# Cutting mixed-width expert segments into equal pieces in a one-core MoE layer

## The chip, the cores and the metric

The kernel runs on one core of one Trainium2 chip. The metric is the device time of one execution in microseconds (us); lower is better.

## The reference, cut to what matters

One layer works on 512 tokens of width 1024. It normalises them, runs a recurrent head group and a long-convolution head group, merges the two, and then passes every token through two of 32 experts. The change lies in that last part:

```python
for e in range(N_EXPERTS):                       # 32 experts, each 1024 -> 512 -> 1024, f32
    ye = (jax.nn.silu(t @ w_gate[e]) * (t @ w_up[e])) @ w_down[e]
    out = out + combine[:, e:e + 1] * ye         # combine is nonzero for two experts of a token
```

Each expert has three matrices of 2 MB (gate, up and down), and every matrix must come from HBM once: 31 experts take part, 195 MB together. A final RMSNorm follows and gives the output.

## The kernel before

**Two phases.** In roughly the first 395 us of the profiled execution the kernel computes the mixing layer and the routing. The rest is the expert phase and a final norm of some 20 us.

**Segments and units.** Experts are sorted by how many tokens they may hold (`CAPS`, 32 to 192 tokens). An expert's tokens are cut into segments of 64 or 32. Segments are packed into units of 128 columns: two of 64, four of 32, or one of 64 and two of 32. A unit gathers its 128 tokens (matmuls of 128x128 bf16 with a one-hot matrix `R`), forms `g` and `u` (eight contraction steps each), multiplies them, transposes, forms `d` in two halves `h` of 512 output columns (four steps each, eight together), and scatters the result back by a one-hot matrix `PT` (matmuls of 128x512 with a `slot` tile as the stationary operand).

There are 14 units. By `ORDER` their groups run F1, F2, M1, M2, H1, M3, Q1, H2, Q2, A, M4, H3, Q3, where A is two units and every other group one. Q1, Q2 and Q3 have four segments of 32. **M4 and H3 have segments of 64, 32 and 32**; all others have two of 64. In M4 the three segments belong to three experts, in H3 the 64 and the first 32 to the same expert.

**The products.** `product` (L1870 and on) walks through the contraction steps. At each step it issues one f32 matmul per segment: the segment's 64 or 32 columns of the tokens are the stationary operand, 512 columns of that expert's weights are streamed, and `tile_position=(0, p0)` puts the segment on its own columns of the array. All of them write one PSUM bank at their own partitions. A chain of start-order edges keeps this sequence in any schedule.

**Weights.** A weight matrix comes in two loads of 1 MB (1024 KB), so an expert takes six. The loads go through a ring of 16 buffers in `slot` and `arena` memory, all issued by SyncE (the SP queue) in one fixed order by the line L1818: 12 for F1, 12 for F2, 12 for each M up to M3, 6 for H1 and H2, 24 for each Q, 12 for A, 18 for M4, 12 for H3. The sixteenth-next load cannot start before the matmuls that read the buffer have run.

**What sets the order.** A recorder notes every operation of the program and a list scheduler (`order`, `forward`, `backward`) places them all, in up to 25 passes, by its own cost table; engines then run in exactly that order. Every recorded operation shows the helper's line L560 (or L567), so tiles and shapes tell the operations apart. Because one plan covers the program, a change of any operation can move instructions everywhere.

Of the kernel before, what the change touches and what calls it, by code (L numbers as in the profile page):

```python
# [742 lines left out]
def kernel(ctx: ExitStack, tc: tile.TileContext, a: dict, out: bass.AP, dbg=None):  # L743
# [45 lines left out]
    def ps():  # L789
        if REC.direct:  # L790
            nbank[0] += 1
            return View.of(Mem((128, 512), F32, banks[nbank[0] % 8]))
        return View.of(Mem((128, 512), F32, bank=-1))
# [11 lines left out]
    def small(name, shape, dt=F32, bufs=1):  # L805
        if name not in rings:
            rings[name] = [0, [cst.tile(shape, dt, name=f"{name}{i}") for i in range(bufs)]]
        r = rings[name]
        r[0] += 1
        return r[1][r[0] % bufs]  # L810
# [807 lines left out]
    def bc(t, shape):  # L1618
        return t.to_broadcast(shape)
# [142 lines left out]
    for g_ in [[first[i:i + 2]] for i in range(0, len(first), 2)] + rest:  # L1762
        assert len(g_) <= 2
        groups.append([])
        for u in g_:
            p0, segs = 0, []
            for s, c in u:
                w = min(64, CAPS[s] - c)
# [83 lines left out]
    def expert_units(subs, need=lambda m: None, then=lambda: None, last=False):  # L1852
        bufs = [(nu[0] + j) % 2 for j in range(len(subs))]
        nu[0] += len(subs)
        for j, (segs, (n, R, iw), wks) in zip(bufs, subs):
            for kb in range(2):
                b = ps()
                for q in range(4):
                    k = 4 * kb + q
                    for r in range(4):  # L1860
                        for m in range(3):
                            T.matmul(b[:, q * n:q * n + n], xp[m][:, r, 128 * k:128 * k + 128], R[:, r, :n],
                                     start=r == 0 and m == 0, stop=r == 3 and m == 2)
                for q in range(4):
                    k = 4 * kb + q
                    xk, bk = XT[j][:, k, :n], b[:, q * n:q * n + n]
                    X.copy(xk, bk, scale=A2k[:, k:k + 1], bias=B2k[:, k:k + 1])
        then()

        def product(sub, m, lhs, parts, c0=0, nc_=512):  # L1870
            b, before = ps(), None
            for i, (k, kk, h) in enumerate(parts):
                for (p0, w), wv in zip(sub[0], sub[2]):
                    o = T.matmul(b[p0:p0 + w, :nc_], lhs[:, k, p0:p0 + w], wv(m, kk, h)[:, c0:c0 + nc_], start=i == 0,
                                 stop=i == len(parts) - 1, tile_position=(0, p0), skip_group_check=True)
                    if not REC.direct:

                        if before is not None:
                            o.preds.setdefault(before, None)
                        before = o.i  # L1880
            return b

        rows = [(k, k % 4, k // 4) for k in range(8)]
        need("g")
        for j, sub in zip(bufs, subs):
            n = sub[1][0]
            bg = product(sub, "g", XT[j], rows)
            S.activation(SG[j][:n], bg[:n], AF.Silu)
        need("u")
        for o in late:  # L1890

            o.like = len(REC.ops)
        late.clear()
        for j, sub in zip(bufs, subs):
            n, sg = sub[1][0], SG[j]
            bu = product(sub, "u", XT[j], rows)
            V.tensor_tensor(sg[:n], sg[:n], bu[:n], op=OP.mult)
            b = ps()
            for q in range(4):
                T.transpose(b[:, q * n:q * n + n], sg[:n, q * 128:(q + 1) * 128], ident[:n, :n])  # L1900
            S.activation(HT[j][:, :, :n], b[:, :4 * n].rearrange("p (q s) -> p q s", q=4), AF.Copy)
        need("d")
        for j, sub in zip(bufs, subs):
            n, R, iw = sub[1]
            iq = small("iq", [128, 4], bufs=2)
            V.scalar_tensor_tensor(iq[:n], bc(iw[:n, 0:1], [n, 4]), 0.25, quart[:n], op0=OP.mult, op1=OP.add)
            V.tensor_tensor(PT[:n], bc(iota[:n, None, :128], [n, 4, 128]), bc(iq[:n, :, None], [n, 4, 128]),
                            op=OP.is_equal)
            n0 = len(REC.ops)
            for h, c0, m in ((0, 0, 512), *((1, *p_) for p_ in (LASTP if last else ((0, 512),)))):  # L1910
                b = product(sub, "d", HT[j], [(k, k, h) for k in range(4)], c0, m)
                cs = slice(512 * h + c0, 512 * h + c0 + m)
                yp = ye[:n, c0:c0 + m]
                V.scalar_tensor_tensor(yp, b[:n, :m], iw[:n, 1:2], g2b[:n, cs], op0=OP.mult, op1=OP.mult)
                if m > 256:
                    S.activation(YH[:n, h, :m], yp, AF.Copy)
                    V.tensor_tensor(YL[:n, :m], yp, YH[:n, h, :m].bitcast(F32), op=OP.subtract)
                for r in range(4):
                    b = ps()
                    if m > 256:  # L1920
                        T.matmul(b[:, :m], PT[:n, r], YH[:n, h, :m], start=True, stop=False)
                        T.matmul(b[:, :m], PT[:n, r], YL[:n, :m], start=False, stop=True)
                    else:
                        T.matmul(b[:, :m], PT[:n, r].bitcast(F32), yp, start=True, stop=True)
                    xs = x2[:, r, cs]
                    V.tensor_tensor(xs, xs, b[:, :m], op=OP.add)
            late.extend(REC.ops[n0:])
# [8 lines left out]
    def need(gi, m):  # L1936

        ss = list(dict.fromkeys(s for i in groups[gi] for _, _, s, _ in units[i]))
        if gi == 1:
            todo = [(s, x, h) for s in ss for x in "gud" for h in range(2)]  # L1940
        else:
            todo = [(s, m, h) for h in range(2) for s in ss]
        for t in todo:
            if t not in loaded:
                loaded.add(t)
                load(*t, LASTP if gi == len(groups) - 1 and t == todo[-1] and m == "d" else ((0, 512),))
# [3 lines left out]
    for gi, g_ in enumerate(groups):  # L1950
        def then(nxt=groups[gi + 1:gi + 2]):
            for i in (nxt[0] if nxt else []):
                unit_place(i)
# [83 lines left out]
```

## Time and profile before

| | |
|---|---|
| median of 3 runs | 927.65 us (925.95 to 929.68) |
| the profiled execution | 931.36 us, of which the span is 929.6 us |
| outside the span | 1.76 us |
| TensorE busy | 855.6 us, 92% of the span |
| VectorE, ScalarE, GpSimd busy | 507.3, 279.9, 23.6 us |
| DMA | 259.73 MB, mean 279 GB/s |
| granted TensorE clock, mean | 0.971 of 2.4 GHz |

Times in the trace count from the start of the span. The tool records each f32 matmul of this kernel as two MATMULs (two passes), so a contraction step of a unit with four 32-wide segments is eight records. Matmuls on different columns of the array overlap in time, so the lengths of records don't add up; the distance from one step's start to the next is what a step costs.

### The profile page before, as it was taken

How to read it: one execution, taken by the hardware profiler on the slowest of the kernel's cores; microseconds unless marked ns; L12 is line 12 of the kernel's file. 1: busy time of each engine (PE TensorE's matmuls, PEld its weight loads, DVE VectorE, ACT ScalarE, POOL GpSimd, SP SyncE). 2: the span in 40 equal slices, each digit the busy share in tenths (PEclk: the TensorE clock that was granted, in tenths of full speed). 3: DMA queues.
4: the chain of work that ended last, by engine and by line, in shares of the span. 5: the costliest groups of instructions: out<-in, count | busy, mean ns of one | idle time of the engine just before them, and what ended most of it. 6: DMA issues, size and time to landing. Idle time of an engine off the chain costs nothing.

```text
span 929.6 us, 13429 instructions
## 1 busy us (share of the span) xinstructions
PE 855.6 (92%) x5282; PEld 453.6 (49%) x5283; DVE 507.3 (55%) x971; ACT 279.9 (30%) x511; POOL 23.6 (3%) x25
## 2 busy tenths in 40 slices
PE   3988998899999799599999999999999999999984
PEld 0344674578887577435544444453554323233332
DVE  7989889599999977604233322431413214212135
ACT  4678188764345124301211110120110100000014
POOL 0000001010003000000000000000000000000002
PEclk9989999799999899799999999999999999999997
DMA  9985377333423596398999989999999999876693
GB/s 292 414 276 195 103 238 218 135 118 120 148 80 131 187 327 223 119 361 306 367 386 386 386 294 359 388 386 386 386 387 386 386 387 382 321 281 223 231 335 142
DMA packets 132618, 259.73 MB, mean 279 GB/s; under 512 B 6928, under 2 KB 28432, under 8 KB 129606
## 3 DMA queue, kind: packets, MB, share of 16 engines
q1 hardware_dynamic: 132534, 258.81, 77.7%
q8 instruction: 43, 0.70, 0.3%
q14 instruction: 25, 0.20, 0.1%
q10 hardware_dynamic: 16, 0.02, 0.0%
HBM read 252.49 MB, written 6.31 MB: 278 GB/s over the span
## 4 chain that ended last, share of the span: by engine, by line
PE 68%; DVE 7%; DMA 1%; ACT 1%; issue 0%; SPq 0%; DVEq 0%; ACTq 0%
PE bank L560 68%; DVE arena L567 2%; DVE slot L567 2%; DVE arena L560 2%; DMA slot<-in_w_down_dram 1%; DVE slot L560 1%; ACT slot L560 0%; DVE R L560 0%; DVE rsb_in L560 0%; DVE fine L560 0%; ACT arena L560 0%; ACT slot L567 0%; SPq L1818 0%; DVE finy L560 0%; DVE hy L560 0%
## 5 line engine op out<-in xcount | busy, mean ns | idle before, releaser
L560 PE MATMUL bank<-arena 128*64 128x512 f32 (+8 forms) x1434 | 314.6, 533 | 26.0 <-DMA arena<-in_b_ada_dram 5.9
L560 PE MATMUL bank<-slot 128*128 128x512 f32 (+1 forms) x1064 | 282.8, 410 | 14.9 <-DVE slot L567 4.8
L560 PE MATMUL bank<-slot,arena 128*64 128x512 f32 (+2 forms) x936 | 242.9, 597 | 1.9 <-DMA slot<-in_w_down_dram 0.9
L560 PEld LDWEIGHTS bank<-slot 128*128 128x128 f32 x1064 | 195.2, 193 | 99.5 <-issue 27.3
L560 PEld LDWEIGHTS bank<-arena 128*32 128x32 f32 (+5 forms) x1434 | 100.5, 132 | 166.8 <-issue 117.5
L560 DVE TENSOR_TENSOR arena<-arena,bank 128x512 f32<-128x512 f32 (+2 forms) x131 | 80.5, 663 | 167.4 <-PE bank L560 167.2
L567 DVE TENSOR_TENSOR arena<-arena 128x512 f32<-128x512 f32 (+3 forms) x142 | 120.6, 886 | 2.5 <-DMA arena<-in_w_dram 1.8
L560 PEld LDWEIGHTS bank<-slot,arena 128*64 128x64 f32 (+1 forms) x936 | 58.3, 124 | 111.6 <-issue 101.0
L560 ACT ACTIVATE arena<-bank 128x512 f32<-128x512 f32 (+1 forms) x66 | 38.3, 595 | 243.4 <-PE bank L560 240.8
L560 PEld LDWEIGHTS <-slot 128*128 128x128 bf16 x1344 | 76.9, 98 | 40.9 <-issue 40.6
L560 PE MATMUL bank<-R,slot 128*128 128x128 bf16 x1344 | 88.7, 220 | 0.3 <-ACT arena L567 0.3
L567 DVE TENSOR_SCALAR arena<-bank,A2c,B2c 128x128 f32<-128x128 f32 x36 | 14.6, 410 | 115.6 <-PE bank L560 115.5
L567 ACT ACTIVATE arena<-bank,B2c,A2c 128x128 f32<-128x128 f32 x76 | 30.7, 454 | 137.1 <-DVE arena L567 85.4
L560 ACT ACTIVATE slot<-arena 128x512 fp32r<-128x512 f32 (+2 forms) x43 | 27.7, 645 | 113.5 <-DVE arena L560 104.2
L560 DVE SCALAR_TENSOR_TENSOR arena<-bank,iw,arena 128x512 f32<-128x512 f32 (+1 forms) x29 | 21.2, 732 | 69.6 <-PE bank L560 69.2
L560 PE MATMUL bank<-ident,arena 128*128 128x128 f32 (+2 forms) x234 | 40.7, 292 | 5.2 <-ACT arena L567 2.2
L560 ACT ACTIVATE arena<-arena 128x512 f32<-128x512 f32 (+6 forms) x59 | 32.7, 589 | 26.5 <-DVE arena L560 21.4
L560 PEld LDWEIGHTS bank<-ident,arena 128*128 128x128 f32 (+2 forms) x234 | 30.2, 160 | 19.9 <-issue 5.7
L567 ACT ACTIVATE slot<-slot 128x1024 fp32r<-128x1024 f32 (+1 forms) x32 | 26.4, 846 | 28.4 <-DVE slot L567 22.9
L567 DVE TENSOR_TENSOR slot<-slot 128x1024 fp32r<-128x1024 f32 (+1 forms) x35 | 33.7, 974 | 0.1
L560 ACT ACT_TABLE_LOAD x23 | 29.5, 1283 | 6.0 <-DMA arena<-in_pack_dram 4.6
L560 DVE TENSOR_TENSOR arena<-bank,arena 128x512 f32<-128x512 f32 (+1 forms) x42 | 27.7, 680 | 5.5 <-PE bank L560 3.1
(172 smaller groups left out, 417.3 us busy)
## 6 DMA issues: line engine op xcount, KB each, us to landing
arena<-in_w_down_dram SPq DMA_DIRECT2D x41, 1024.0 KB, 13.5
slot<-in_w_up_dram SPq DMA_DIRECT2D x39, 1024.0 KB, 14.0
slot<-in_w_gate_dram SPq DMA_DIRECT2D x32, 1024.0 KB, 13.6
arena<-in_w_gate_dram SPq DMA_DIRECT2D x30, 1024.0 KB, 11.8
arena<-in_w_up_dram SPq DMA_DIRECT2D x23, 1024.0 KB, 9.4
slot<-in_w_down_dram SPq DMA_DIRECT2D x20, 1024.0 KB, 10.3
arena<-in_w_ada_dram SPq DMA_DIRECT2D x32, 512.0 KB, 5.1
slot<-in_w_ada_dram SPq DMA_DIRECT2D x8, 1024.0 KB, 11.1
```

The source lines that it names most:

```text
L560: return self.rec.add(self.name, lambda: f(*[real(v) for v in args], **{k: real(v) for k, v in kw.items()}), outs, ins, cost, **x)
L567: return cost, lambda: f(*[real(v) for v in args], **{k: real(v) for k, v in kw.items()}), port
```

## The change

`product` now takes the smallest segment width of the unit, `one`, and cuts every segment into pieces of that width. A piece starts at partition `p` and uses the weights of the segment that it came from. In a unit whose segments are all equally wide, each segment is one piece and nothing changes. In M4 and H3 the 64-wide segment becomes two 32-wide pieces, so a step has four matmuls of 32 columns in place of one of 64 and two of 32.

```diff
             b, before = ps(), None
+
+            one = min(w for _, w in sub[0])
+            turns = [(p, one, wv) for (p0, w), wv in zip(sub[0], sub[2]) for p in range(p0, p0 + w, one)]
             for i, (k, kk, h) in enumerate(parts):
-                for (p0, w), wv in zip(sub[0], sub[2]):
+                for p0, w, wv in turns:
                     o = T.matmul(b[p0:p0 + w, :nc_], lhs[:, k, p0:p0 + w], wv(m, kk, h)[:, c0:c0 + nc_], start=i == 0,
```

**Place 1: TensorE, the end of the `g` product of unit M4.** `bank_70` (before) and `bank_74` (after) is the product's PSUM bank, `slot` and `arena` name where the weights lie, and the size is that of the output. Before:

```order
L560 MATMUL bank_70<-slot,arena 64x512
L560 MATMUL bank_70<-arena 32x512 x2
L560 MATMUL bank_70<-arena 64x512
L560 MATMUL bank_70<-slot,arena 32x512 x2
L560 MATMUL bank_70<-arena 64x512
L560 MATMUL bank_70<-slot,arena 32x512 x2
L560 MATMUL bank_73<-slot 128x512
```

After:

```order
L560 MATMUL bank_74<-arena 32x512 x2
L560 MATMUL bank_74<-slot,arena 32x512 x2
L560 MATMUL bank_74<-arena 32x512 x4
L560 MATMUL bank_74<-slot,arena 32x512 x2
L560 MATMUL bank_74<-arena 32x512 x2
L560 MATMUL bank_74<-slot,arena 32x512 x2
L560 MATMUL bank_70<-slot 128x512
```

The product keeps its place between the down products and the scatter (128x512 from `slot`) of unit A; a step is now four outputs of 32 rows, with no other width between them.

**Place 2: TensorE, the `u` product of unit H3.** Before, `bank_74` is `u`; the rows between are scatters of unit M4 (128x512):

```order
L560 MATMUL bank_73<-slot 128x512
L560 MATMUL bank_69<-slot 128x512
L560 MATMUL bank_74<-slot,arena 32x512 x2
L560 MATMUL bank_74<-slot,arena 64x512
L560 MATMUL bank_74<-slot,arena 32x512 x2
L560 MATMUL bank_68<-slot 128x512
```

After, `bank_70` is the end of H3's `g`, `bank_71` the start of its `u`, and `bank_72` gathers tokens for Q3:

```order
L560 MATMUL bank_72<-R_137,slot 128x128
L560 MATMUL bank_70<-slot,arena 32x512 x13
L560 MATMUL bank_71<-slot,arena 32x512 x3
L560 LDWEIGHTS slot
L560 MATMUL bank_72<-R_137,slot 128x128
```

The steps stand in runs of four, with few other instructions cut in; the runs of H3's `g` and `u` alternate with the gathers of the unit that follows.

**Place 3: the SP queue, in the first phase.** One piece of the difference; `gd`, `w_ada`, `w_u` and `x` belong to the mixing layer:

```order
+L560 DMA arena<-in_w_ada_dram 128x4x256 x3
+L560 DMA gd<-arena 128x512 x2
 L560 DMA slot<-in_x_dram 128x1024
-L560 DMA gd<-arena 128x512
-L560 DMA arena<-in_w_ada_dram 128x4x256
-L560 DMA gd<-arena 128x512
-L560 DMA arena<-in_w_ada_dram 128x4x256
-L560 DMA gd<-arena 128x512
-L560 DMA arena<-in_w_ada_dram 128x4x256
```

The plan of the first phase, which the edit does not touch, has been made anew too. The order of the expert weights' loads among themselves is the same.

## Rows read from the trace of the kernel before

**Rows 1.** The page: span, busy time, and DMA by 40 slices.

```profile
span 929.6 us, 13429 instructions
...
PE 855.6 (92%) x5282; PEld 453.6 (49%) x5283; DVE 507.3 (55%) x971; ACT 279.9 (30%) x511; POOL 23.6 (3%) x25
...
GB/s 292 414 276 195 103 238 218 135 118 120 148 80 131 187 327 223 119 361 306 367 386 386 386 294 359 388 386 386 386 387 386 386 387 382 321 281 223 231 335 142
```

**Rows 2.** Windows of the expert phase: busy us by engine, granted clock, DMA.

```profile
395.00:465.00 70.00, 70.00 (x482) 32.53 (x478) 18.75 (x41) 10.13 (x21) 0.00 (x0) 1.00 0.95 345
465.00:720.00 255.00, 253.94 (x2009) 118.44 (x2009) 81.98 (x168) 34.06 (x71) 0.00 (x0) 1.00 1.02 376
720.00:757.00 37.00, 37.00 (x172) 12.79 (x168) 8.96 (x16) 4.98 (x9) 0.00 (x0) 1.00 1.05 386
757.00:790.20 33.20, 32.90 (x106) 9.19 (x104) 11.35 (x18) 1.86 (x3) 0.00 (x0) 1.00 1.05 383
790.20:907.20 117.00, 113.73 (x659) 36.73 (x657) 26.38 (x45) 10.67 (x21) 0.00 (x0) 1.00 0.78 279
907.20:929.60 22.40, 9.96 (x77) 5.90 (x77) 12.02 (x46) 10.89 (x34) 4.97 (x4) 0.77 0.37 134
```

**Rows 3.** The chain that ended last, from 776 us on: start, length, what.

```profile
776.25 119.12 PE bank L560 x630
896.49 10.68 DMA slot<-in_w_down_dram
907.21 6.96 PE bank L560 x63
```

**Rows 4.** Waits of the SP queue, longest in total: us, times, longest.

```profile
SPq L1818 <- PE bank L560: 324.7, 109, 13.4
```

**Rows 5.** SP timeline: issue of expert weights from M4's first load on.

```profile
720.11 1.48 SPq L1818 DMA_DIRECT2D slot<-in_w_gate_dram  x1
...
765.12 2.38 SPq L1818 DMA_DIRECT2D arena<-in_w_down_dram  x1
768.33 5.10 SPq L1818 DMA_DIRECT2D arena<-in_w_gate_dram  x2
773.68 5.00 SPq L1818 DMA_DIRECT2D slot<-in_w_gate_dram  x2
784.43 12.58 SPq L1818 DMA_DIRECT2D slot<-in_w_up_dram  x4
...
809.10 0.38 SPq L1818 DMA_DIRECT2D arena<-in_w_gate_dram  x1
...
896.49 3.01 SPq L1818 DMA_DIRECT2D slot<-in_w_down_dram  x3
```

**Rows 6.** PE timeline, M4's `g` product: start, length, shape, records.

```profile
757.51 1.05 PE L560 MATMUL bank<-arena 128*32 128x512 f32 x4
758.49 1.07 PE L560 MATMUL bank<-slot,arena 128*64 128x512 f32 x2
759.49 1.05 PE L560 MATMUL bank<-arena 128*32 128x512 f32 x4
760.48 1.07 PE L560 MATMUL bank<-slot,arena 128*64 128x512 f32 x2
761.48 1.05 PE L560 MATMUL bank<-arena 128*32 128x512 f32 x4
```

**Rows 7.** PE timeline, H3's `u` product, its last six steps.

```profile
843.53 11.98 PE L560 MATMUL bank<-slot,arena 128*64 128x512 f32 x36
855.44 0.25 PE L560 MATMUL bank<-auxb,R 128*128 128x3 bf16 x4
```

**Rows 8.** PE timeline, a down product of Q3, with four segments of 32.

```profile
900.53 0.60 PE L560 MATMUL bank<-slot,arena 128*32 128x512 f32 x2
900.54 1.00 PE L560 MATMUL bank<-arena 128*32 128x512 f32 x2
900.96 0.60 PE L560 MATMUL bank<-slot,arena 128*32 128x512 f32 x2
900.97 1.00 PE L560 MATMUL bank<-arena 128*32 128x512 f32 x2
901.38 0.60 PE L560 MATMUL bank<-slot,arena 128*32 128x512 f32 x2
```

**Rows 9.** PE timeline, two-of-64 steps of unit A: all pieces of one width.

```profile
711.28 9.66 PE L560 MATMUL bank<-slot,arena 128*64 128x512 f32 x44
720.88 1.42 PE L560 MATMUL bank<-slot 128*128 128x512 f32 x5
```

**Rows 10.** PE timeline, one 32-wide matmul alone on the array.

```profile
667.40 1.05 PE L560 MATMUL bank<-slot,arena 128*32 128x512 f32 x2
668.37 0.50 PE L560 MATMUL bank<-slot 128*128 128x512 f32 x1
```

**Rows 11.** Groups of weight loads into the array, by form: busy us, mean ns.

```profile
L560 PEld LDWEIGHTS bank<-slot,arena 128*32 128x32 f32 x440 | 20.5, 110 | 40.1 <-issue 32.8 <-DMA slot<-in_w_ada_dram 2.6 <-DMA slot<-in_w_down_dram 1.7
```

**Rows 12.** Windows with a busy array fed by DMA, and with an idle one.

```profile
607.00:700.00 93.00, 91.94 (x826) 45.21 (x821) 25.16 (x52) 13.64 (x30) 0.00 (x0) 1.00 1.05 386
372.00:388.00 16.00, 4.87 (x54) 4.17 (x54) 13.83 (x53) 4.84 (x7) 0.39 (x2) 0.57 0.48 166
```

**Rows 13.** Timeline of the tail: after the last weights, and the first output store.

```profile
907.21 1.05 PE L560 MATMUL bank<-slot,arena 128*32 128x256 f32 x4 [0.86 <-DMA slot<-in_w_down_dram]
908.19 0.73 PE L560 MATMUL bank<-slot 128*128 128x512 f32 x2
908.73 2.52 DVE L560 TENSOR_TENSOR arena<-arena,bank 128x512 f32<-128x512 f32 x4 [2.67 <-PE bank L560]
...
919.93 4.47 SPq L560 DMA_DIRECT2D out_dram<-slot  x8
```

## The prediction

> **What bounds the kernel now.** I read the page first. TensorE is busy for 92% of the span, while the other engines stay under 56%. The GB/s line by slices runs at 386 to 388 for long stretches, and then drops to 321, 281, 223 and 231 near the end [rows 1]. So there are two candidates, the array and the weight stream. The windows tell which one holds where. From 465 to 790 us both are near full: the array has no idle time worth naming and the loads run at 376 to 386 GB/s. From 790.2 to 907.2 us the array is still busy for 113.7 of 117.0 us, but the loads run at 279 GB/s [rows 2]. In that stretch the array alone is the bound. The chain of waits says the same: 119 us of TensorE from 776 us on, then one weight load of 10.7 us, then the last matmuls [rows 3]. The SP queue confirms it from the other side: issues of expert weights (L1818) waited 324.7 us in 109 waits for matmuls to give buffers back [rows 4]. The reader should see there that loads are late because buffers come free late.
>
> Which work makes the array slow there? M4's first load is issued at 720.1 us and Q3's first at 809.1 us [rows 5], and M4's products start at 757 us [rows 6]. So M4 and H3, the two units that the edit touches, fill the stretch from 757 to about 875 us, just where the loads fall behind.
>
> **What a step costs.** In M4's `g`, the pattern of a pair of records of 64 and four of 32 repeats from 757.51 to 761.48 us in two steps, so a step takes 1.985 us [rows 6]. In H3's `u`, 36 records, six steps, lie between 843.53 and 855.44 us: 1.985 us again [rows 7]. In a unit with four segments of 32, the four matmuls of one pass start together, and the next pass starts 0.43 us later (900.53, 900.96, 901.38): 0.86 us for the two passes of a step [rows 8]. With two segments of 64, 44 records or 11 steps take 9.60 us, 0.87 us each [rows 9]. So equal widths share the array completely. In the mixed step the 64 goes alone, the two 32s go together, and each of the two changes of width adds about 0.13 us: 2 x 0.86 + 2 x 0.13 = 1.98.
>
> The Trainium skill ("TensorEngine Tiling (Array Packing)", Key Properties) says that a change of tiling mode drains the array, while tiles of one mode run independently. The 1.985 against 0.86 us agrees with it.
>
> **The change part by part.** *Array work.* M4 and H3 have 8 steps for `g`, 8 for `u` and 2 x 4 for `d`, so 48 steps together. Before: 48 x 1.985 = 95.3 us. After, each step is four matmuls of 32, the form of rows 8, so 48 x 0.86 = 41.3 us. That is 54.0 us less. It adds one matmul a step, 48 in all, which costs nothing of its own as long as the four lie side by side. If a run begins or ends inside a step, a piece may stand alone on the array, and that takes 0.97 us [rows 10]. The order shows about a dozen such places in M4's and H3's products, so at most 12 us come back. The array's saving is 42 to 54 us.
>
> *What the end gains.* The loads can't follow that far. From 757 to 907.2 us the array works 32.9 + 113.7 = 146.6 us; after the change 93 to 105 us are left. In the same time 33.2 us x 383 + 117.0 us x 279 GB/s = 45.4 MB arrive [rows 2], which at 386 GB/s needs 117.5 us. The array would be done 13 to 25 us ahead of its weights, so the weight stream becomes the bound, and the gain is what the stream can make up. Before 790.2 us there is nothing to make up, since it ran at 383 to 386. After it, 117.0 x 279 = 32.6 MB would take 84.6 us at 386 GB/s: 32.4 us less. In the longest stretch in which the ring worked beside a busy array the rate was 376 [rows 2]; at that the 32.6 MB take 86.8 us, 30.2 us less. I take 376, because a queue that waits now and then is what this kernel has shown over a long stretch.
>
> Can the loads be issued in time? The ring has 16 buffers, and a load takes about 2.7 us at 386 GB/s. At 765 to 784 us the queue issued only the first loads of H3, in bursts [rows 5]; each waited for M4's `g` and `u` to give a buffer back. After the change M4's `g` takes 7 us in place of 16, so these buffers come free before their turn. While the array waits for weights it consumes each load soon after it lands. With some five loads on their way (13 us of queue at 2.7 us each) about ten buffers are then free, an estimate. So I see no stall in that stretch.
>
> *The tail.* From the last landing at 907.2 us to the end are 22.4 us [rows 2, 3]. The last two down products, their scatters and the final norm stay. Two small effects oppose each other. The adds of the first half's scatter, 2.5 us on VectorE after the last landing [rows 13], can come earlier, since the array is no longer behind. On the other hand the array will pause between the last loads, and its clock can fall: where it was busy for 4.9 of 16 us, the granted clock was 0.57, so much of that stretch ran at 1.2 GHz [rows 12]. I leave the tail at 22.4 us.
>
> *The rest of the program.* The planner has placed everything anew, the first phase too, and the SP queue there has another order. No row prices that. I take nothing for it and let it widen the range by some 10 us, about 2.5% of that phase's 395 us; this width is a choice.
>
> **The sum.** 931.36 - 30.2 = 901.2 us for an execution like the profiled one. That one stands 3.7 us above the median, so against the median it is 927.65 - 30.2 = **897.5 us**.
>
> **The rivals.**
>
> *The stream also closes its earlier gaps (0.10).* From 395 to 465 us it ran at 345 GB/s [rows 2]. At 386 these 24.2 MB take 62.6 us, 7.4 us less. With the full 32.4 us, and 2.5 us from the tail, the time is 927.65 - 42.3 = 885 us. Against it: the units there are unchanged, so only a luckier order could do this.
>
> *Part of the gain is given back (0.19).* With idle time on the array its clock may fall in Q3 and in the tail, and the first phase may come out longer. The tail's 10 us of matmuls at half rate would cost about 7 us; with some 8 us in the first phase the gain shrinks to 15 us, 912 us. For it: the row of 0.57 above. Against it: from 607 to 700 us, which is a stretch of Q work with loads at full rate, the clock stayed at 1.00 and the array busy, because the planner fills the waits with gathers [rows 12].
>
> *The weight loads into the array don't hide (0.03).* Eight loads of 32 columns a step at 0.110 us each [rows 11] would, if nothing covered them, make the step 0.86 + 0.88 = 1.74 us. Then 48 x 0.245 = 12 us are saved, and the array stays the bound: 916 us. Against it: rows 8 have just this form, with its eight loads, at 0.86 us. The Trainium skill ("TensorE: Matmul & The Clock Gate", The mechanism, in the part on packing small matmuls) says that a weight load overlaps running matmuls only when its row group differs, which pieces side by side in columns don't fulfil; the trace disagrees, since the step of 0.86 us is the two passes alone.
>
> *The pieces take turns in time and not side by side (0.03; the other side).* If four pieces that stream the same expert's weights, or four short issues in a row, can't run together, a step is 4 x 0.97 = 3.9 us at the row of one 32-wide matmul alone [rows 10]. That is 48 x 1.9 = 91 us more on the array, and about 1019 us in all. It decides as soon as the step is over 1.985 us, that is when fewer than about two pieces run at a time. Against it: Q units run four at a time [rows 8]. In unit A, whose steps take 0.87 us [rows 9], the two segments of the first unit share one expert's weights.
>
> The forecast itself gets 0.65. The range of 886 to 911 us leaves out about 2 in 10: the low rival and the far part of the give-back. Within 0.5% of the time before (about what a measurement of this kernel can tell from no change) I see 0.02, slower 0.03 and faster 0.95.
>
> **What would show it.** In the profile after, M4's and H3's steps should start every 0.86 us. The slices between 780 us and the last weights should read about 380 GB/s or more, and the chain there should name DMA landings of expert weights, not only TensorE. TensorE's busy time should fall by some 45 us, with idle time whose releaser is DMA. The last weights should land near 877 us, some 22 us before the end. I am wrong if a step still takes 1.7 us or more, if the loads stay under 350 GB/s although the steps are fast (then buffers are the limit and not the stream), or if the first expert matmuls start some 10 us later than before, which would put the blame on the first phase.

## The result, and the profile after

The changed kernel takes 890.93 us (median of 4 runs, 890.72 to 891.2). The kernel before took 928.52 us beside it (925.95 to 929.68). The ratio is 0.960, with a 95% interval of 0.958 to 0.962: 37.6 us faster. That is inside the range, and 6.6 us below the time that was predicted.

The page of the changed kernel answers to [rows 1]:

```profile
span 888.9 us, 13625 instructions
...
PE 810.6 (91%) x5378; PEld 449.6 (51%) x5379; DVE 508.2 (57%) x980; ACT 273.9 (31%) x499; POOL 22.4 (3%) x26
...
GB/s 290 415 313 261 60 204 217 209 94 142 166 48 131 136 349 187 252 213 387 272 387 386 386 354 300 385 386 387 386 386 386 386 386 387 386 386 385 387 382 130
```

TensorE has 45 us less to do. The dip of the GB/s line near the end is gone: the stream stays at 382 to 387 up to the last slice but one.

The windows of the changed kernel, cut at the same events as [rows 2] (M4's products start at 748 us now, the last weights are used from 864.6 us on):

```profile
395.00:465.00 70.00, 70.00 (x494) 33.16 (x491) 23.62 (x50) 9.53 (x20) 0.00 (x0) 1.00 0.96 350
465.00:748.00 283.00, 281.94 (x2126) 127.73 (x2123) 85.34 (x172) 39.04 (x80) 0.00 (x0) 1.00 1.03 377
748.00:864.60 116.60, 106.53 (x854) 42.70 (x852) 36.80 (x64) 12.13 (x23) 0.00 (x0) 0.97 1.05 386
864.60:888.90 24.30, 11.48 (x84) 7.13 (x84) 12.52 (x47) 10.91 (x34) 4.96 (x4) 0.78 0.42 150
```

From 748 to 864.6 us the loads run at 386 GB/s, and the array has 10 us of idle time. What sets the end of this stretch shows in the chain of waits; compare [rows 3]:

```profile
759.18 55.73 PE bank L560 x504
...
850.59 13.99 DMA arena<-in_w_down_dram
864.63 8.48 PE bank L560 x70
```

The unbroken 119 us of TensorE before the last load are 56 us now. Between the lines shown the chain goes on through shorter pieces of TensorE (18 us), VectorE and ScalarE up to 838.7 us, and from there it runs through the issues of the SP queue and the last load. M4's `g` product on the timeline, against [rows 6]:

```profile
748.77 0.60 PE L560 MATMUL bank<-slot,arena 128*32 128x512 f32 x2
748.78 0.60 PE L560 MATMUL bank<-arena 128*32 128x512 f32 x2
749.20 0.60 PE L560 MATMUL bank<-slot,arena 128*32 128x512 f32 x2
749.21 0.60 PE L560 MATMUL bank<-arena 128*32 128x512 f32 x2
749.63 0.60 PE L560 MATMUL bank<-slot,arena 128*32 128x512 f32 x2
```

Four pieces start within 0.01 us, and the next pass 0.43 us later: 0.86 us a step, as in the units of four 32s [rows 8]. And the array now waits for weights in Q3's `u` and down products, of which the rows of before have one, of 0.86 us [rows 13]:

```profile
842.94 1.05 PE L560 MATMUL bank<-arena 128*32 128x512 f32 x2 [0.94 <-DMA arena<-in_w_up_dram]
845.65 1.05 PE L560 MATMUL bank<-arena 128*32 128x512 f32 x2 [1.67 <-DMA arena<-in_w_up_dram]
848.37 6.58 PE L560 MATMUL bank<-arena 128*32 128x512 f32 x26 [1.67 <-DMA arena<-in_w_up_dram]
...
864.63 1.05 PE L560 MATMUL bank<-arena 128*32 128x256 f32 x4 [1.66 <-DMA arena<-in_w_down_dram]
```

**Where the 40.7 us of the span went.** Three marks divide both spans: the issue of A's first load (686.10 before, 677.64 after), the first matmul on the last weights (907.21 and 864.63) and the end. The first part is 8.5 us shorter, the second 34.1 us (221.1 to 187.0), and the third 1.9 us longer. So the stretch that the edit touches gave about what was forecast (34.1 us, less 1.9 in the tail, for the 30.2), and the first part, which the edit doesn't touch, gave 8.5 us on top.

**The theories.** Mine: the faster steps relieve the array by 42 to 54 us, the stream lets some 32 us of it through (this limit is the cap below: the weights can't arrive sooner), and the earlier start comes from the new plan of the first phase. Rivals: the new order of the expert phase, not the pieces, gives the gain; or there is no cap, and the pieces save only some 32 us.

### The profile page after: what moved, and what is told of

It reads as the page before. It is cut to its first block, busy times and chain, and to the rows that moved or that the text cites. A ratio compares the mean times of both kernels' runs of the same rounds, so it can differ in the third digit from the quotient of the medians.

```text
span 888.9 us, 13625 instructions
## 1 busy us (share of the span) xinstructions
PE 810.6 (91%) x5378; PEld 449.6 (51%) x5379; DVE 508.2 (57%) x980; ACT 273.9 (31%) x499; POOL 22.4 (3%) x26
## 4 chain that ended last, share of the span: by engine, by line
PE 61%; DVE 11%; DMA 2%; SPq 1%; issue 1%; ACT 1%; ACTq 0%
PE bank L560 61%; DVE arena L567 4%; DVE arena L560 3%; DVE slot L567 2%; DMA arena<-in_w_down_dram 2%; SPq L1818 1%; DVE slot L560 1%; ACT slot L560 0%; DVE R L560 0%; DVE rsb_in L560 0%; DVE fine L560 0%; ACT arena L560 0%; DVE finy L560 0%; ACT arena L567 0%; DVE he L560 0%
## 5 line engine op out<-in xcount | busy, mean ns | idle before, releaser
L560 PE MATMUL bank<-arena 128*32 128x512 f32 (+7 forms) x1474 | 300.1, 536 | 31.8 <-DMA arena<-in_b_ada_dram 7.3
L560 PE MATMUL bank<-slot 128*128 128x512 f32 (+1 forms) x1064 | 276.5, 404 | 12.8 <-DVE slot L567 7.5
L560 PEld LDWEIGHTS bank<-slot 128*128 128x128 f32 x1064 | 191.8, 189 | 97.6 <-issue 29.9
L560 PE MATMUL bank<-slot,arena 128*32 128x512 f32 (+2 forms) x992 | 220.5, 595 | 1.0 <-DMA slot<-in_w_ada_dram 0.6
L560 PEld LDWEIGHTS bank<-arena 128*32 128x32 f32 (+4 forms) x1474 | 101.2, 132 | 157.6 <-issue 98.8
L560 PEld LDWEIGHTS bank<-slot,arena 128*32 128x32 f32 (+1 forms) x992 | 57.7, 122 | 87.7 <-issue 78.8
L567 ACT ACTIVATE arena<-bank,B2c,A2c 128x128 f32<-128x128 f32 x75 | 30.3, 454 | 138.6 <-DVE arena L567 83.8
L567 ACT ACTIVATE slot<-slot 128x512 fp32r<-128x512 f32 (+1 forms) x29 | 24.0, 839 | 28.8 <-DVE slot L567 23.1
L567 DVE TENSOR_TENSOR slot<-arena,slot 128x512 fp32r<-128x512 f32 (+5 forms) x25 | 27.8, 1113 | 1.9 <-ACT hy L560 1.3
```

Source lines behind the costliest of these rows:

```text
L560: return self.rec.add(self.name, lambda: f(*[real(v) for v in args], **{k: real(v) for k, v in kw.items()}), outs, ins, cost, **x)
L567: return cost, lambda: f(*[real(v) for v in args], **{k: real(v) for k, v in kw.items()}), port
```

## The experiments

Each kernel ran in several rounds beside the kernel before; a gain is against that. "The stretch" is the time from A's first load to the issue of the last expert load, 211.6 us in the kernel before and 181.0 us in the changed one. The expectations also measure from A's long run, the 44 records in a row of [rows 9], to the first matmul on the last weights: 195.9 us before (711.28 to 907.21) and 161.7 us in the changed kernel (702.95 to 864.63).

### The old plan with pieces, and the new plan without

In the first kernel the planner sees the old operations; only when one is issued does it become two (the edit is shortened):

```diff
+ one = min(w_ for _, w_ in sub[0])
+ if w > one:                       # what the planned operation issues
+     def cut(...):
+         for p in range(p0, p0 + w, one):
+             nc.tensor.matmul(b[p:p + one], lhs[:, k, p:p + one], ..., tile_position=(0, p))
+     o.fn = cut
```

> The plan is that of the kernel before, instruction for instruction; only when M4's and H3's 64-wide matmuls are issued, each becomes two of 32. Theory (the faster steps give the gain of the last stretch, up to what the weight stream can make up; the 8.3 us by which unit A started earlier in the changed kernel come from the new plan of the first phase): A's long run starts at about 711 us as before, the stretch from there to the last landing shrinks from 195.9 to 162 to 166 us, the tail stays at 22 to 24 us, and the time is some 30 to 33 us below before. Rival (the new order of the expert phase gives most of the gain, the pieces little): the stretch stays above 180 us and the gain under 15 us.

Measured: 898.0 us against 929.18, ratio 0.967 (0.965 to 0.969), 31.2 us faster. Windows of this kernel, from A's first load to the last, and from there to the end:

```profile
684.70:865.60 180.90, 168.11 (x1281) 69.91 (x1272) 54.13 (x103) 19.37 (x37) 0.00 (x0) 0.97 1.04 383
865.60:896.50 30.90, 16.58 (x124) 8.33 (x124) 13.97 (x49) 12.11 (x36) 4.98 (x4) 0.85 0.59 211
```

A's long run starts at 710.22 us and the last weights are used from 874.19 us on: 164.0 us, as expected of the theory. With the plan held fixed, the pieces alone give the whole of the stretch's gain (180.9 us, against 181.0 in the changed kernel). The rival that the new order of the expert phase does it falls.

The second kernel does the reverse: planned as pieces, issued whole (of the edit, the line that says what is issued).

```diff
- turns = [(p, one, wv) for ...]
+ turns = [(p, one, wv, w if p == p0 else 0) for ...]    # first piece issues all of w, second nothing
```

> The plan is that of the changed kernel, made for pieces; but where it has the two pieces of a 64-wide segment, the segment is issued whole at the first and nothing at the second. Theory: A's long run starts near 703 us as in the changed kernel, M4's and H3's steps take about 2 us again, the stretch to the last landing is back at 190 to 200 us, and the time is some 5 to 10 us below before: the part that the plan of the first phase gives by itself. Rival (the new order of the expert phase gives most of the gain): the stretch stays under 175 us and the gain is 25 us or more.

Measured: 938.84 us, 9.7 us slower than before (ratio 1.012, 1.009 to 1.014). A's long run starts at 702.38 us, so the first phase is indeed 9 us shorter here too. But the stretch is not back at its old length, it is longer:

```profile
677.10:903.00 225.90, 224.05 (x1185) 75.27 (x1177) 54.26 (x103) 19.16 (x37) 0.00 (x0) 1.00 0.83 305
```

My number was a miss: I expected a gain of 5 to 10 us. The plan that is made for pieces breaks runs inside a step, and with whole segments a pair of 32s is torn apart at such a place. The order of this kernel shows it in M4's `u` (`bank_71`; `L1883` issues the whole segment):

```
L560 MATMUL bank_71<-arena 32x512
L1883 MATMUL bank_71<-slot,arena 64x512
L560 MATMUL bank_71<-arena 32x512
L560 MATMUL bank_69<-slot 128x512
L560 MATMUL bank_74<-slot 128x512
L560 MATMUL bank_71<-arena 32x512
```

Each 32 stands alone between a 64 and other work, where two would share the array. In M4's and H3's products the trace of this kernel has 20 matmuls of 32 columns that start alone, ten torn pairs; the kernel before has none. At the 0.97 us of one alone [rows 10] and 0.86 us of a pair, ten pairs cost 10 x (2 x 0.97 - 0.86) = 10.8 us, an estimate, out of the 14.3 us by which the stretch is longer. The rest stays open. The rival falls here too: the new order gives nothing by itself.

### One unit at a time

```diff
- turns = [(p, one, wv) for (p0, w), wv in ... for p in range(p0, p0 + w, one)]
+ turns = [(p, one if cut else w, wv) for (p0, w), wv in ... for p in range(p0, p0 + w, one if cut else w)]
```

`cut` holds for M4 alone, or for H3 alone.

> Only unit M4 is cut into pieces, H3 keeps 64, 32 and 32. Theory: the array is relieved of 27 us, less than the 34 us that the stream could make up, so the stretch from A's long run to the last landing shrinks by 20 to 27 us (169 to 176 us), more than half of the 34 us of the full change. The first phase is planned anew and may move the total by 8 us either way. Rival (there is no cap by the stream, and what the array saves is halved for some other reason): the stretch shrinks by half of 34 us, 17 us.

> Only unit H3 is cut into pieces, M4 keeps 64, 32 and 32. Theory: 27 us less on the array, and the stretch from A's long run to the last landing shrinks by 20 to 27 us; together with the run that cuts M4 alone the two shrink it by 40 us or more, over the 34 us of both at once. Rival (no cap, the two add): 17 us, so that the two make up 34 us.

Measured: with M4 alone 904.4 us (ratio 0.974), with H3 alone 898.79 us (0.968), both against 929.18. The windows, M4 alone and then H3 alone:

```profile
678.60:870.10 191.50, 191.21 (x1222) 70.52 (x1215) 53.80 (x102) 19.48 (x37) 0.00 (x0) 1.00 0.99 361
```

```profile
679.00:863.60 184.60, 183.93 (x1203) 69.72 (x1202) 53.71 (x101) 18.90 (x36) 0.00 (x0) 1.00 1.02 375
```

The stretch shrinks by 20.1 and 27.0 us, 47.1 us together, while both at once give 30.6 us. By the marks of the expectation (A's long run to the last weights, 195.9 us before) it is 177.3 and 172.1 us, 18.7 and 23.8 us less and 42.5 together; M4 alone misses its 20 by a little. With one unit cut the array has hardly any idle time (191.2 of 191.5 us busy) and the stream is at 361 and 375 GB/s; with both, the stream is at its 386 and the array waits. Effects that don't add, with the bound changing sides, are what a cap looks like. The rival, two effects that add up to 34 us, falls by the sum.

### The cap lifted

Both kernels with twelve loads fewer: two of Q3's experts use the weights of the other two. So the output leaves those two experts' own weights out.

```diff
+ SAME = {29: 27, 30: 28}
- ss = list(dict.fromkeys(s for i in groups[gi] ...))
+ ss = list(dict.fromkeys(SAME.get(s, s) for i in groups[gi] ...))
```

> The kernel before, with twelve loads left out: two of Q3's four experts are not loaded, and their segments are computed with the weights of the other two. The array's work stays the same, the stream has 12 MB, 32.6 us, less after M4. Theory (the array alone is the bound here): hardly faster than before, by 0 to 5 us from the end, plus up to 8 us if the new plan of the first phase is the shorter one. Rival (the stream is the bound before too): 20 us or more faster in the stretch from A's first load to the end.

> The changed kernel with the same twelve loads left out. Theory (the array is relieved of 42 to 54 us, and the stream's cap hides a part of it): with the cap lifted, the stretch from A's first load to the end is 42 to 52 us shorter than in the run that leaves out the same loads from the kernel before, clearly more than the 32 us by which the two full kernels differ there. Rival (the pieces save only some 32 us on the array, and there is no cap): again 30 to 34 us.

Measured: 926.64 us for the kernel before with fewer loads (ratio 0.997, 0.995 to 0.999), and 876.22 us for the changed one (0.942), both against 929.51. The windows from A's first load to the end, before and then changed:

```profile
682.50:923.90 241.40, 225.87 (x1275) 78.59 (x1267) 69.90 (x152) 28.47 (x66) 5.12 (x4) 0.98 0.71 262
```

```profile
684.90:875.10 190.20, 172.31 (x1311) 72.04 (x1309) 67.81 (x146) 28.14 (x65) 5.14 (x4) 0.97 0.90 330
```

Taking 32.6 us off the stream gives the kernel before 2.9 us: the array alone bound it. With the same loads gone, the pieces shorten this stretch by 51.2 us, while between the two full kernels it is 243.5 - 211.3 = 32.2 us. So the array's relief is near 51 us, and the stream hides some 19 us of it. In the changed kernel with fewer loads the stream still runs at 386 GB/s up to its last load (684.9 to 830.7 us), beside an array that is busy for 143.8 of these 145.8 us; a little more relief may be hidden there.

### Pieces everywhere

The first kernel of this list, with `one` taken as 32 in all units, so that 216 more steps run as four pieces in the same plan:

```diff
- if w > one:
+ if w > 32:
```

> The plan of the kernel before; at issue every 64-wide matmul of every unit becomes two of 32, so the nine units of two 64s also run four pieces a step, on top of M4 and H3. Theory (pieces of one width share the array, their weight loads hide): the same time as the run that cuts only M4 and H3 in this plan, within 3 us, with a step of 0.86 us in every unit. Rival (each extra piece costs its weight load or its issue, 0.1 to 0.2 us a step, unseen in M4 and H3 because the stream is the bound): 216 steps make 20 to 45 us more on the array, and the time is 10 us or more above that run.

Measured: 898.05 us, against 898.0 with M4 and H3 alone. From M1's first load to A's, where the array is busy throughout and a cost of the pieces would show, both kernels take 271.8 us (412.1 to 683.9, and 412.9 to 684.7). The rows of a `g` or `u` run of unit A on this kernel's timeline (L1880 is the line that issues the pieces):

```profile
735.98 7.93 PE L1880 MATMUL bank<-arena 128*32 128x512 f32 x72
743.84 0.66 PE L560 MATMUL bank<-ident,arena 128*128 128x128 f32 x4
```

72 records, nine steps of four pieces, take 743.84 - 735.98 = 7.86 us, 0.87 us a step, the same as two of 64 [rows 9]. An extra piece costs nothing that this can measure. That settles the rival of weight loads that don't hide, and of pieces of one expert that can't run side by side.

### Another plan without the edit

The planner of the kernel before may not keep its first passes' plans; what it takes then has the changed kernel's order on the SP queue in the first phase.

```diff
- if new[0] < best[0]:
+ if n >= 2 and (n == 2 or new[0] < best[0]):
```

> The kernel before without the edit; only the planner may not keep the plans of its first passes, and so takes one whose order in the first phase is that of the changed kernel on the SP queue. Theory (the 7 to 8 us by which the expert phase starts earlier in the changed kernel are a property of that plan): the first expert load is issued at 305 to 308 us, unit A's at 677 to 680 us, and the time is 5 to 9 us below before. Rival (the earlier start needs the pieces): A's first load at 685 us and the time of before.

Measured: 924.54 us, 5.0 us faster than before (ratio 0.993, 0.991 to 0.996). The first expert load is issued at 308.61 us and A's at 679.38 us, and the stretch is as before:

```profile
679.40:890.90 211.50, 211.20 (x1179) 72.48 (x1171) 54.00 (x101) 18.95 (x36) 0.00 (x0) 1.00 0.89 327
```

So the earlier start needs no pieces. It belongs to the plan. The first load comes 0.6 us later than I expected, and the gain is at the low end of my 5 to 9 us. The 31.2 us of the pieces and these 5.0 us make 36.2 of the 37.6 us; the last 1.4 us are not assigned.

### Half the changes of width

The kernel before without pieces; every other step takes its segments in reverse.

```diff
- for (p0, w), wv in zip(sub[0], sub[2]):
+ for (p0, w), wv in list(zip(sub[0], sub[2]))[::-1 if i % 2 else 1]:
```

> The kernel before without pieces; only every other step of a product takes its segments in reverse (64, 32, 32, then 32, 32, 64), so the width changes once a step and not twice. Theory (a step of 1.985 us is two passes of 0.86 us one behind the other and about 0.13 us for each change of width): a pair of steps in an unbroken run takes 3.70 us and not 3.97, the array has 6 us less to do, and the stretch from A's first load to the last load's issue is 5 to 7 us shorter than 211.6. Rival (the 64 and the 32s simply last that long next to each other, whatever their order): pairs of 3.97 us and the same stretch.

Measured: 925.8 us against 928.92, ratio 0.998 (0.996 to 1.000): the total is not settled. The timeline of M4's `g` in this kernel is:

```profile
752.67 1.91 PE L560 MATMUL bank<-arena 128*32 128x512 f32 x8
754.51 1.93 PE L560 MATMUL bank<-slot,arena 128*64 128x512 f32 x4
756.37 1.91 PE L560 MATMUL bank<-arena 128*32 128x512 f32 x8
```

A pair of steps takes 756.37 - 752.67 = 3.70 us, in place of 2 x 1.985 = 3.97, and the stretch is 205.0 us, 6.6 us less. So 0.13 us for a change of width is right, and the rest of a mixed step, 1.72 us, is two widths one behind the other. Of the 54 us, 48 x 0.26 = 12.5 us were changes of width and 41 us the sharing of the array.

### Another order of the units

If the stream is the bound at the end, its earlier gaps are worth something. Units with many loads for their array time come earlier here.

```diff
- ORDER = "MMHMQHQAMHQ"
+ ORDER = "MQMMHMHQAQH"      # and, in the second kernel, "MQMHMMHHQAQ"
```

> The changed kernel with the units after F2 in another order: M, Q, M, M, H, M, H, Q, A, Q, H. The units that need many loads for their array time (Q: 24 loads, 65 us of stream for some 34 us of array) come earlier, so the stream, which is now the bound at the end, is kept full from the first units on. Theory (the cap is the stream, and some of its time is lost while F, M and H units hold the 16 buffers): 8 to 18 us below the changed kernel. Rival (ring and planner lose as much elsewhere): within 5 us of it.

> The same idea with a Q unit at the end as now: M, Q, M, H, M, M, H, H, Q, A, Q. Theory: 8 to 18 us below the changed kernel, like the run that ends with an H unit, since only the stream's total counts. Rival: within 5 us of the changed kernel.

Measured: 895.95 us (ratio 0.965, 0.962 to 0.969) for the first and 885.14 us (0.954, 0.950 to 0.957) for the second, against 928.92. Both keep the stream full from 465 us on. The windows of the second:

```profile
395.00:465.00 70.00, 70.00 (x499) 34.03 (x496) 22.60 (x47) 9.74 (x21) 0.00 (x0) 1.00 0.96 346
465.00:700.00 235.00, 235.00 (x1815) 107.21 (x1813) 75.74 (x152) 30.28 (x60) 0.00 (x0) 1.00 1.05 386
700.00:850.00 150.00, 147.76 (x1118) 62.67 (x1116) 50.96 (x95) 15.36 (x30) 0.00 (x0) 1.00 1.05 386
```

At 386 in place of 375 GB/s (the changed kernel from 465 to 700 us), 235 us of stream are 6.7 us shorter, and the kernel is 5.8 us faster than the changed one's 890.93 (which was timed on another occasion; the ratios to the kernel before lie just apart). That is less than the 8 to 18 us I expected: behind 465 us only one gap was left to close, and the one from 395 to 465 us stayed (346 GB/s).

The first order is a plain miss: I expected 8 to 18 us below the changed kernel, and it is 5.0 us above it. Its stream gains as much: from the first expert load to the last it takes 546.4 us and the second order 547.5, in place of 552.6. It gives this away at both ends. Its first expert load is issued at 313.0 us in place of 306.0, under another plan of the first phase, and from the last load's issue to the end it takes 35.5 us in place of 30.3. I put that down to its last unit, an H with much array work for its loads; no run shows it apart. The kernel with the order M, Q, M, H, M, M, H, H, Q, A, Q beats both kernels.

## Why the prediction was right, and where it was off

**The step.** Predicted 0.86 us in place of 1.985; the timeline shows 0.86, and the run with half the changes of width confirms how 1.985 is made up.

**The array's relief.** Predicted 42 to 54 us; 51 us with the cap lifted. TensorE's busy time fell by 45.0 us, as forecast; the prediction gives no working for its 45, apart from the 42 to 54 us. With the cap lifted it fell by 51.4 us (852.4 to 801.0). Two things in the changed kernel's trace go with the lower figure, though no run prices them. Six matmuls of 32 columns ran alone in M4's and H3's products. And from 847.5 to 854.3 us, while the array waited for weights again and again (the rows at 842.94, 845.65 and 848.37 us), the granted clock was 0.50, that is 1.2 GHz.

**The cap.** The decisive step, that the weight stream and not the array sets the gain, held. I took 376 GB/s, for 30.2 us; the stream ran at 386 in the changed kernel and at 383 with the old plan. With the old plan held, the last weights were used 31.6 us earlier relative to A's first load (221.1 to 189.5 us), between my two values and nearer to the 32.4 us at 386. The 376 was the wrong row: it averages a stream at 386 with one gap (294 and 359 GB/s in two slices of [rows 1]), and at the end no such gap came. My picture of the ring was off as well. I estimated ten free buffers, but from 748 to 865 us the queue's loads still waited for matmuls 27 times, 49.2 us in all. No wait was longer than 3.9 us, and the stream stayed at 386; in the kernel before, from 790 to 907 us, 16 waits took 88.7 us, up to 11.5 us each, and the stream fell to 279.

**The tail.** Left at 22.4 us; it was 24.3 us in the changed kernel and 22.3 us with the old plan. Of the 1.9 us, 1.5 are TensorE's part of the chain behind the last weights, 8.48 us in place of 6.96. The clock took nothing from the tail: it was granted at 0.78, against 0.77 before, and in both it fell only after the last matmul. In the stretch it was granted at 0.97, and where it was low, from 847.5 to 854.3 us, the loads ran at 387 GB/s.

**The rest of the program.** The term I took for nothing was 5 us by the run without pieces, and 8.5 us in the two profiles (6.7 us of it shown by that run's profile; executions of one plan differ by 1.4 us there, 686.1 and 684.7). It is most of the 6.6 us between forecast and result; the pieces' own gain, 31.2 us with the old plan in place of 30.2, is another 1.0 us, and under 1 us is not assigned. The sign was not to be had from the rows: nothing in the profile of one plan prices another. That the new plan helped, where the give-back rival had it cost 8 us, was luck.

**The rivals.** The early gaps of the stream stayed: 350 GB/s from 395 to 465 us and 377 up to M4, against 345 and 376 before; what came on top of the cap is the plan's earlier start. The clock fell for a while, but no time given back by it shows. The weight loads hide, and the pieces run side by side.

## What to carry to other kernels

When an edit relieves the bound engine, work out how far the next bound lets it: here 51 us on the array became 32 us, and the bytes left divided by the full rate gave 32.4 us before any run, though I forecast with a lower rate. Take the rate for it from a stretch where the stream is the bound, not from one where it waits for buffers. In a program whose order one planner makes, an edit at the end can move the beginning by half a per cent or more; issue the edited work under the old plan to tell the two apart.

## What was not expected

A plan made for four pieces is bad for whole segments: the same work, issued whole in that plan, took 938.84 us, against 929.18 in its own plan (ratio 1.012). And cutting all 64-wide matmuls into two of 32 cost nothing that these runs measure: with 6243 TensorE weight loads in place of 5379 the time was the same (898.05 and 898.0 us).
